# Five score banks, norms beside the attention values, and joint Q and K sums in a cosine-similarity attention kernel

## The chip, the cores and the metric

The kernel runs on one core of a Trainium2 chip. The metric is device microseconds (us) of one execution; the median of three runs before the change is 190.02 us (189.93 to 190.08). The profile is of one execution of its own, and its numbers are used as durations.

## The reference

Eight batches of twelve heads, 512 positions of 64 elements, fp32 in and out, tau = 0.1:

```python
Q_norm = Q / (np.linalg.norm(Q, axis=-1, keepdims=True) + 1e-10)
K_norm = K / (np.linalg.norm(K, axis=-1, keepdims=True) + 1e-10)
scores = np.einsum('bhqd,bhkd->bhqk', Q_norm, K_norm) / tau
weights = np.exp(scores - np.max(scores, axis=-1, keepdims=True))
weights = weights / (np.sum(weights, axis=-1, keepdims=True) + 1e-10)
return np.einsum('bhqk,bhkd->bhqd', weights, V).astype(np.float32)
```

The scores are cosines over tau, at most 10, so the kernel leaves the maximum out.

## The kernel before

The 96 heads are taken as 48 pairs (0 to 47); a pair fills 128 partitions with two heads of 64. For each pair s the work is a chain of named operations:

- LD loads Q (s,0) and K (s,1), LV loads V: 256 KB each, all issued by SyncE (SP), in one queue and in the order written out for it. ST stores the result. For pair 0 the loads are halves, K's from ScalarE's queue.
- SQ (L368) squares Q and K in one GpSimd (POOL) instruction; VC (L575, POOL) casts V to bf16 into `vb`, whose 65th column is one.
- The sum of squares of K is made on TensorE by SSQ (L385, eight matmuls against the identity, 64 columns, into unused columns of a value bank) and finished by a VectorE reduction of 64 elements (RED, L392). That of Q is a VectorE reduction of 512 elements (RED, L396). Pairs 1 to 3 have both on TensorE; pairs 43 and 47 both on VectorE.
- NEW (L419 to L430) are the Newton steps of the inverse square root for a group of one, two or four pairs on VectorE; the norms stand in a PSUM bank of their own (`nps`).
- SCL (L451) scales Q (VectorE) and K (POOL, for some pairs VectorE); TR (L457) transposes on TensorE into `tps`; EVA (L465, VectorE) copies that to `qt`.
- SCO (L551) makes scores on TensorE: two 64x512 matmuls, one for each head, into two of the four banks of `scps`. EXP (L567) is the exponential on ScalarE (ACT) over both banks, 1024 elements, from PSUM to `et`. A pair has four of these.
- PV (L587) multiplies with V: for each head h four steps of four matmuls of 65 columns, into value bank h of `ops`; RCP (L599) and NRM (L604) on VectorE divide by the 65th column into `ob`.

One chunk, (43, 3), has its exponential as a polynomial on VectorE and POOL. The program is straight-line: `ORDER` is a table that holds for each engine the numbers of all operations in the order in which it runs them. Each engine and the SP queue work strictly in this order, and an operation waits (through semaphores) for those that it needs. SCO of a bank waits for the EXP that read it last; VC waits for its LV; PV waits for all EXP of its pair, for VC, and for the NRM that last read its bank. In the table for SP the number 197 is the load of V of pair 4, 238 or 239 that of pair 5. Buffers are rings: 17 of Q and K, 8 of loaded V, 16 of cast V.

Of the kernel before, what the change touches and what calls it, by code (L numbers as in the profile page):

```python
# [108 lines left out]
def bass_cosine_similarity_attention_kernel(  # L109
# [26 lines left out]
    et = [sb(f"et{i}", [128, NT, 2, SEQ], bf16) for i in range(R_ET)]  # L136
# [21 lines left out]
    n_ps = nc.alloc_psum_tensor("nps", [128, R_X, MOST], f32)  # L158
# [34 lines left out]

    P.add("one", "pool", "one", -100, [], lambda e: e.memset(ones[:, :], 1.0))
# [31 lines left out]
    session, attached, early = {}, {}, []  # L226
    for s, w in sorted(((s, w) for s in range(NP) for w in range(2) if on_pe(s, w)), key=lambda j: (due_red(j[0]), j)):
        at = due_red(s) + 0.3
        if s < EARLY:
            early.append((s, w))  # L230
            continue
        due, i, h = next(x for x in slots if x[0] >= at and (x[1], x[2]) not in attached)
        attached[i, h] = (s, w)
# [93 lines left out]

    def pair(s):
# [74 lines left out]
        reds = [("RED", i, w) for i in range(first[g], first[g] + sizes[g]) for w in range(2)]  # L403
# [14 lines left out]
        elif s == first[g]:  # L418
# [17 lines left out]
            for k in news(g):  # L436
                needs = [done] if k else reds + [("SCL", i, w) for i in past for w in range(2) if w == 0 or i in K_ON_DVE]
                if k == 0 and g == R_X:
# [3 lines left out]
                done = ("NEW", g, k)  # L442
                P.add(done, "dve", "new7" if k == 7 and on_dve else "new", TF - 4.9 - slack(s, M_NEW) + (M_STEP * (k - 7) if s > 8 else 0.23 * k), needs, steps[k])

        for w in range(2):
# [81 lines left out]
    def rest(s):  # L527
# [3 lines left out]
        for c in range(NT):  # L531
# [14 lines left out]
            turn = chunks.index((s, c))  # L546
            b = turn % 2

            def sco(e, c=c, b=b):
                for h in range(2):  # L550
                    last = e.matmul(  # L551
                        out=sc_ps[:, 2 * b + h, :], lhsT=qt[iqt][64 * h : 64 * h + 64, 1, c, :],
                        rhs=qt[iqt][64 * h : 64 * h + 64, 0, :, :], start=True, stop=True)
                return last

            used = [("EXP", 0, 2 * c + i, 1) for i in range(2)] if turn < NT + 2 else exps(*chunks[turn - 2])
            P.add(("SCO", s, c), "pe", "sco", T0 + 0.9 * c, [("EVA", s)] + used, sco)
            if last_pair and c == NT - 1:
                for k, (h, lo, hi) in enumerate(PIECES):
                    P.add(("EXP", s, c, k), "act", "exp1" if hi - lo == NT else "exph", T0 + 0.9 * c + 0.3 * k,  # L560
                          [("SCO", s, c)] + [key("PV", s - R_ET, i, NT - 1) for i in range(2)],
                          lambda e, c=c, b=b, h=h, q=slice(128 * lo, 128 * hi): e.activation(
                              out=et[iet][:, c, h, q], in_=sc_ps[:, 2 * b + h, q], func=ACT.Exp, scale=math.log(2.0) / UNIT if group[s] in poly_groups else inv_tau))
                continue
            P.add(("EXP", s, c), "act", "exp", T0 + 0.9 * c,
                  [("SCO", s, c)] + [key("PV", s - R_ET, h, NT - 1) for h in range(2)] + ["table"],
                  lambda e, c=c, b=b: e.activation(  # L567
                      out=et[iet][:, c, :, :], in_=sc_ps[:, 2 * b : 2 * b + 2, :],
                      func=ACT.Exp, scale=math.log(2.0) / UNIT if group[s] in poly_groups else inv_tau))
# [12 lines left out]
        for h in range(2):  # L582
            for i in range(NT):
                def pv(e, h=h, i=i):
                    for c in range(NT):
                        t = i
                        last = e.matmul(  # L587
                            out=o_ps[h][:, 65 * t : 65 * t + 65],
# [6 lines left out]
            grid = o_ps[h][:, 0 : 65 * NT].rearrange("p (t x) -> p t x", x=65)  # L595
# [230 lines left out]
```

## Time and profile before

| | |
|---|---|
| median of three runs | 190.02 us |
| span of the profiled execution | 189.64 us |
| busy, share of the span | ACT 182.2 us (96%), PE 175.8 (93%), DVE 169.5 (89%), POOL 160.7 (85%) |
| moved by DMA | 50.76 MB, mean 268 GB/s |

PE is TensorE, PEld its weight loads, DVE VectorE, ACT ScalarE, POOL GpSimd, SPq the DMA queue that SP issues. The profiled execution stands 0.38 us below the median of the runs. "L567 ACT ... x186 | 170.9, 1182 | 0.7" reads: 186 instructions of line 567 kept ACT busy for 170.9 us in all, one of them takes 1182 ns (they overlap), and ACT was idle 0.7 us in front of them.

### The profile page before, as it was taken

The numbers are of one execution on the slowest core, as the hardware profiler recorded it, in microseconds if no ns is written. First come the engines' busy times: TensorE is split into PE (matmuls) and PEld (weight loads), VectorE is DVE, ScalarE is ACT, GpSimd is POOL, SyncE is SP. The second block draws the span as 40 slices with busy tenths as digits, with TensorE's granted clock in tenths as the row PEclk, the third lists the DMA queues.
The fourth block names the chain that finished last, engine by engine and source line by source line (L and its number), as shares of the span: only waits on it lengthen the run. The fifth ranks groups of instructions, "written<-read, shape, count | busy, mean of one in ns | idle before, by whom it ended". The sixth has DMA issues, their size and how long they took to land.

```text
span 189.6 us, 6661 instructions
## 1 busy us (share of the span) xinstructions
PE 175.8 (93%) x2705; PEld 111.0 (59%) x2705; DVE 169.5 (89%) x541; ACT 182.2 (96%) x215; POOL 160.7 (85%) x149
## 2 busy tenths in 40 slices
PE   8798899999999999999899989999999899899992
PEld 2455456566665666666466656556666566555652
DVE  1779999999999999999899998999989999998752
ACT  5699999999999999999999999999999999999993
POOL 5599998999999999999999999999999994594000
PEclk9979999999999999999999999999999999999999
DMA  5999999998997898899999999996983062200655
GB/s 163 340 352 350 349 348 370 365 367 256 301 363 253 246 337 296 258 351 309 368 379 319 359 360 368 361 341 194 313 295 119 3 221 79 94 0 3 203 188 168
DMA packets 52446, 50.76 MB, mean 268 GB/s; under 512 B 3136, under 2 KB 52416, under 8 KB 52416
## 3 DMA queue, kind: packets, MB, share of 16 engines
q1 hardware_dynamic: 51984, 50.02, 80.1%
q8 instruction: 21, 0.34, 0.7%
q10 hardware_dynamic: 432, 0.33, 0.5%
q14 instruction: 9, 0.07, 0.1%
HBM read 37.75 MB, written 12.58 MB: 265 GB/s over the span
## 4 chain that ended last, share of the span: by engine, by line
ACT 73%; PE 8%; DMA 5%; POOL 5%; DVE 3%; SPq 2%; issue 1%; DVEq 0%
ACT et L567 73%; DMA out_dram<-ob 3%; DMA qk<-in_Q_dram 3%; PE ops L587 2%; PE scps L551 2%; POOL sq L368 2%; POOL vb L575 2%; POOL qn L451 2%; PE ops L385 1%; SPq L345 1%; PE tps L457 1%; PE scps L540 1%; DVE ob L604 1%; SPq L342 0%; PE ops L619 0%
## 5 line engine op out<-in xcount | busy, mean ns | idle before, releaser
L567 ACT ACTIVATE et<-scps 128x1024 bf16<-128x1024 f32 x186 | 170.9, 1182 | 0.7 <-PE scps L551 0.6
L368 POOL TENSOR_TENSOR sq<-qk 128x1024 bf16<-128x1024 f32 x44 | 82.6, 1893 | 0.2 <-DMA qk<-in_K_dram 0.2
L551 PE MATMUL scps<-qt 64*128 64x512 bf16 x374 | 73.0, 386 | 7.0 <-ACT et L567 4.1
L587 PE MATMUL ops<-vb,et 128*128 128x65 bf16 x1504 | 75.7, 195 | 1.0 <-DVE ob L604 0.6
L587 PEld LDWEIGHTS ops<-vb,et 128*128 128x128 bf16 x1504 | 57.3, 98 | 30.4 <-issue 18.4
L451 POOL TENSOR_TENSOR qn<-qk,rk 128x512 bf16<-128x512 f32 x38 | 39.2, 1042 | 7.1 <-DVE rk L426 7.0
L604 DVE TENSOR_TENSOR ob<-ops,rd 128x256 f32<-128x256 f32 x94 | 39.1, 420 | 1.5 <-DMA out_dram<-ob 0.8
L451 DVE TENSOR_TENSOR qn<-qk,nps 128x512 bf16<-128x512 f32 x56 | 36.9, 679 | 0.7 <-ACT nps L412 0.6
L465 DVE COPY qt<-tps 128x1024 bf16<-128x1024 bf16 x47 | 32.2, 684 | 0.8 <-PE tps L457 0.6
L457 PE MATMUL tps<-ident,qn 128*128 128x128 bf16 x376 | 32.3, 221 | 0.3 <-DVE qn L451 0.2
L551 PEld LDWEIGHTS scps<-qt 64*128 64x128 bf16 x374 | 18.4, 92 | 23.7 <-ACT et L567 8.3
L396 DVE TENSOR_REDUCE xs<-sq 128x8 f32<-128x512 bf16 x46 | 30.5, 673 | 0.2 <-POOL sq L368 0.2
L575 POOL TENSOR_SCALAR vb<-vf 128x512 bf16<-128x512 f32 x48 | 28.9, 619 | 0.0
L457 PEld LDWEIGHTS tps<-ident,qn 128*128 128x128 bf16 x376 | 21.8, 98 | 10.0 <-issue 5.0
L599 DVE RECIPROCAL rd<-ops 128x4 f32<-128x4 f32 x94 | 16.3, 176 | 5.0 <-PE ops L587 3.8
L385 PE MATMUL ops<-sq,ident 128*128 128x64 bf16 x384 | 19.5, 196 | 0.2 <-DVE qt L298 0.2
L385 PEld LDWEIGHTS ops<-sq,ident 128*128 128x128 bf16 x384 | 14.7, 99 | 4.3 <-issue 3.0
L392 DVE TENSOR_REDUCE xs<-ops 128x8 f32<-128x64 f32 x46 | 9.7, 210 | 0.8 <-PE ops L385 0.7
L419 DVE TENSOR_TENSOR ts<-xs,nps 128x32 f32<-128x32 f32 (+2 forms) x34 | 6.6, 194 | 0.6
L426 DVE SCALAR_TENSOR_TENSOR nps<-ts,nps 128x32 f32<-128x32 f32 (+3 forms) x34 | 6.7, 196 | 0.5
L422 DVE SCALAR_TENSOR_TENSOR ts<-ts,nps 128x32 f32<-128x32 f32 (+2 forms) x34 | 6.5, 192 | 0.4
L362 POOL TENSOR_TENSOR sq<-qk 128x512 bf16<-128x512 f32 (+1 forms) x5 | 4.7, 954 | 2.4 <-DMA qk<-in_K_dram 2.1
(60 smaller groups left out, 52.8 us busy)
## 6 DMA issues: line engine op xcount, KB each, us to landing
vf<-in_V_dram SPq DMA_DIRECT2D x48, 256.0 KB, 6.2
qk<-in_Q_dram SPq DMA_DIRECT2D x47, 256.0 KB, 5.2
qk<-in_K_dram SPq DMA_DIRECT2D x47, 256.0 KB, 6.2
out_dram<-ob SPq DMA_DIRECT2D x47, 256.0 KB, 5.7
qk<-in_Q_dram SPq DMA_DIRECT2D x2, 128.0 KB, 2.7
qk<-in_K_dram ACTq DMA_DIRECT2D x2, 128.0 KB, 2.9
out_dram<-ob SPq DMA_DIRECT2D x1, 128.0 KB, 1.7
out_dram<-ob ACTq DMA_DIRECT2D x1, 64.0 KB, 1.8
```

What stands on the lines that cost most here:

```text
L368: lambda e: e.tensor_tensor(out=sqf, in0=data, in1=data, op=ALU.mult))
L385: last = e.matmul(out=o_ps[bank][:, 320:384], lhsT=ident[:, :], rhs=sq[iqs][:, 8 * w : 8 * w + 8, 8 * k : 8 * k + 8], start=(k == 0), stop ...
L396: lambda e, w=w, dst=dst: e.tensor_reduce(out=dst, in_=sq[iqs][:, 8 * w : 8 * w + 8, :], axis=AX.X, op=ALU.add))
L451: lambda e, w=w, r=r: e.tensor_tensor(out=qn[iqn][:, w].rearrange("p t h d -> p h t d"), in0=qk[iq][:, w].rearrange("p h (t d) -> p h t d" ...
L457: last = e.transpose(t_ps[:, w, t, :], qn[iqn][:, w, t].rearrange("p h d -> p (h d)"), ident[:, :])
L465: lambda e: e.tensor_copy(out=qt[iqt][:, :, :, :].rearrange("p w t x -> p (w t x)"), in_=t_ps[:, :, :, :].rearrange("p w t x -> p (w t x)")))
L551: last = e.matmul(out=sc_ps[:, 2 * b + h, :], lhsT=qt[iqt][64 * h : 64 * h + 64, 1, c, :], rhs=qt[iqt][64 * h : 64 * h + 64, 0, :, :], sta ...
L567: lambda e, c=c, b=b: e.activation(out=et[iet][:, c, :, :], in_=sc_ps[:, 2 * b : 2 * b + 2, :], func=ACT.Exp, scale=math.log(2.0) / UNIT i ...
L575: lambda e: e.tensor_scalar(out=vb[:, ivb : ivb + n, :, :, 0:DIM].rearrange("p n h c d -> p (n h c) d"), in0=vf[:, iv : iv + n].rearrange( ...
L587: last = e.matmul(out=o_ps[h][:, 65 * t : 65 * t + 65], lhsT=et[iet][:, c, h, 128 * t : 128 * t + 128], rhs=vb[:, ivb, h, c, :], start=(c ...
L599: lambda e, h=h, grid=grid: e.reciprocal(out=rd[io][:, h, :], in_=grid[:, :, DIM]))
L604: lambda e, h=h, grid=grid: e.tensor_tensor(out=ob[io][:, h], in0=grid[:, :, 0:DIM], in1=rd[io][:, h, :].unsqueeze(2).to_broadcast([128, N ...
```

## The change

**Exponentials.** `scps` has five banks. Up to pair 7 all stays in units of two tiles of 512; from pair 8 on `exp_groups` cuts the run of tiles into units of three and two in turn (banks 0 to 2 and 3 to 4), across pairs where `et`, now one tensor, allows it. SCO makes a unit's tiles, EXP takes them in one instruction of 1536 or 1024 elements. There are 156 EXP of these instead of 186: 60 of three tiles and 96 of two. A unit still has the same score banks as the unit before the last.

**Norms.** The bank of `nps` is given up for this. The norms of the first groups (pairs 0 to 7) stand in score bank 4 until it is needed; those of later groups in the last columns of value bank 1. So that TensorE does not write the bank while VectorE uses it, each NEW and each SCL on VectorE stands in a window: after NRM of head 1 of one pair, and PV of head 1 of the next pair waits for it (`in_window`).

**Sums.** For pairs 4 to 19 Q and K are summed together: SSQ has eight matmuls of 128 columns, RED reduces 128 elements, and the reduction of 512 goes. K of pairs 20 and 21 is now summed on VectorE, K of 43 and 47 on TensorE. All sums go to value bank 0.

**Rings and order.** The ring of Q and K has 16 buffers instead of 17, that of cast V 14 instead of 16. The tables of all engines are new.

```diff
-    sc_ps = nc.alloc_psum_tensor("scps", [128, 4, SEQ], f32)
+    sc_ps = nc.alloc_psum_tensor("scps", [128, 5, SEQ], f32)
...
-    n_ps = nc.alloc_psum_tensor("nps", [128, R_X, MOST], f32)
+    n_ps = both[:, :, 512 - 2 * MOST : 512].rearrange("p b (r x) -> p b r x", x=MOST)
+    n_head = sc_ps[:, 4, :].rearrange("p (r x) -> p r x", x=MOST)
...
+    def together(s, dst, g):
+        bank, due, before = session[s, 1]
+
+        def ssq(e):
+            for k in range(8):
+                last = e.matmul(
+                    out=o_ps[bank][:, 260:388], lhsT=ident[:, :], rhs=sq[s % R_SQ][:, :, 8 * k : 8 * k + 8],
+                    start=(k == 0), stop=(k == 7))
+            return last
...
+    def in_window(key, w, b):
+
+        if w < 0:
+            window_ops.setdefault((0, b), []).append(key)
+            return [("RED", s, 1) for s in range(1, ONE_BANK)]
+        window_ops.setdefault((w + 1, b), []).append(key)
+        return [("NRM", w, b)]
...
+        def sco(e):
+            for i, (s, c, h) in enumerate(halves):
+                last = e.matmul(
+                    out=sc_ps[:, bank + i, :], lhsT=qt[s % R_QT][64 * h : 64 * h + 64, 1, c, :],
+                    rhs=qt[s % R_QT][64 * h : 64 * h + 64, 0, :, :], start=True, stop=True)
+            return last
...
+        P.add(("EXP", u), "act", {1: "exp1h", 2: "exp", 3: "exp3"}[n], T0, [("SCO", u), "table"] + free,
+              lambda e: e.activation(out=et_all[:, at : at + n, :], in_=sc_ps[:, bank : bank + n, :], func=ACT.Exp, scale=scale))
...
+    for (s, b), keys in window_ops.items():
+        P.ops["PV", s, b, 0].needs += keys
...
-BY_VECTOR = (43, 47)
+BY_VECTOR = (20, 21)
...
-RINGS = (17, 8, 16, 6, 4, 4, 5, 8, 3)
+RINGS = (16, 8, 14, 6, 4, 4, 5, 8, 3)
...
+FIRST_WIDE = 8
+HEAD_GROUPS = 5
...
+SUMMED_TOGETHER = (4, 5, 6, 7, 8, 9, 10, 11, 12, 13, 14, 15, 16, 17, 18, 19)
...
     "sp": (
-        "6 7 69 70 108 109 10 151 152 71 195 196 110 237 238 153 271 272 197 313 314 239 347 348 273 389 390 315 "
...
+        "6 7 69 70 108 109 10 151 152 71 195 196 110 236 237 153 269 310 384 311 270 343 385 344 416 738 487 312 "
+        "386 557 596 629 415 457 526 458 456 238 488 417 668 558 150 527 197 669 271 811 345 68 770 699 597 630 "
```

Where the tables move instructions, three places matter below. The first is SP's queue. Before, V of pair 4 is its 19th transfer (the second `vf` row here; the first and third are V of pairs 3 and 5; the two halves of pair 0 count as two):

```order
L342 DMA qk5<-in_Q_dram 128x2x256
L342 DMA qk5<-in_K_dram 128x2x256
L345 DMA vf<-in_V_dram 128x2x256
L342 DMA qk6<-in_Q_dram 128x2x256
L342 DMA qk6<-in_K_dram 128x2x256
L345 DMA vf<-in_V_dram 128x2x256
L342 DMA qk7<-in_Q_dram 128x2x256
L342 DMA qk7<-in_K_dram 128x2x256
L345 DMA vf<-in_V_dram 128x2x256
```

After, V of pair 4 is the 45th transfer, the last row here; the other two `vf` rows are V of pairs 5 and 10, and `qk1` is already pair 17:

```order
L383 DMA qk11<-in_Q_dram 128x2x256
L386 DMA vf<-in_V_dram 128x2x256
L383 DMA qk12<-in_K_dram 128x2x256
L386 DMA vf<-in_V_dram 128x2x256
L383 DMA qk1<-in_Q_dram 128x2x256 [waits s_act]
L383 DMA qk14<-in_K_dram 128x2x256
L685 DMA out_0_dram<-ob2 128x2x256 [waits s_dve]
L383 DMA qk13<-in_K_dram 128x2x256
L386 DMA vf<-in_V_dram 128x2x256
```

V of pair 4 has moved 26 transfers back, behind loads of Q and K of pairs 7 to 17 and of Q of pair 19, V of pairs 5, 7, 9, 10 and 11, and the store of pair 2 (`ob2`).

The second is POOL, around the cast of V of pair 4 (it waits for `d_v4`, the arrival of that load). Before:

```order
L575 TENSOR_SCALAR vb<-vf 128x8x64 [waits d_v3]
L368 TENSOR_TENSOR sq2<-qk8 128x1024 [waits d_qk8]
L575 TENSOR_SCALAR vb<-vf 128x8x64 [waits d_v4]
L575 TENSOR_SCALAR vb<-vf 128x8x64 [waits d_v7]
L451 TENSOR_TENSOR qn2<-qk6,rk2 128x2x4x64 [waits s_pe,s_dve]
L451 TENSOR_TENSOR qn3<-qk7,rk2 128x2x4x64 [waits s_pe]
L368 TENSOR_TENSOR sq3<-qk9 128x1024 [waits d_qk9]
L368 TENSOR_TENSOR sq4<-qk10 128x1024 [waits d_qk10]
```

After:

```order
L409 TENSOR_TENSOR sq2<-qk8 128x1024 [waits d_qk8]
L409 TENSOR_TENSOR sq3<-qk9 128x1024 [waits d_qk9]
L501 TENSOR_TENSOR qn2<-qk6,rk2 128x2x4x64 [waits s_pe,s_dve]
L501 TENSOR_TENSOR qn3<-qk7,rk2 128x2x4x64 [waits s_pe]
L409 TENSOR_TENSOR sq4<-qk10 128x1024 [waits d_qk10]
L652 TENSOR_SCALAR vb<-vf 128x8x64 [waits d_v4]
L652 TENSOR_SCALAR vb<-vf 128x8x64 [waits d_v5]
L409 TENSOR_TENSOR sq5<-qk11 128x1024 [waits d_qk11]
L501 TENSOR_TENSOR qn0<-qk8,rk0 128x2x4x64 [waits s_pe,s_dve]
```

The cast has moved behind the squares of pairs 9 and 10, and the squares of pair 11 stand behind it.

The third is PE, where PV of pair 4 begins, after the transposes of pair 7 (`qn3`) and between two SCO of pair 6 (`qt2`). Before:

```order
L551 MATMUL scps<-qt2 128x512 [waits s_act]
L551 MATMUL scps<-qt2 128x512
L457 MATMUL tps<-ident,qn3 128x128 [waits s_dve]
L457 MATMUL tps<-ident,qn3 128x128 x3
L587 MATMUL ops<-vb,et4 128x65 [waits s_dve]
L587 MATMUL ops<-vb,et4 128x65 x7
L551 MATMUL scps<-qt2 128x512 [waits s_act]
L551 MATMUL scps<-qt2 128x512
```

After:

```order
L507 MATMUL tps<-ident,qn3 128x128 x4
L664 MATMUL ops<-vb,et 128x65 [waits s_dve,s_pool]
L664 MATMUL ops<-vb,et 128x65 x7
L550 MATMUL scps<-qt2 128x512 [waits s_act]
L550 MATMUL scps<-qt2 128x512
L664 MATMUL ops<-vb,et 128x65 x8
L664 MATMUL ops<-vb,et 128x65 [waits s_dve]
L664 MATMUL ops<-vb,et 128x65 x7
```

The place is the same, but PV of pair 4 now has a wait for POOL of its own, for the cast. The SCO behind it (`qt2`, third unit of pair 6) feeds the 23rd two-tile exponential.

More of the change, by code (lines that the diff above doesn't have):

```diff
@@ L437, in pair @@
                 needs = [done] if k else reds + [("SCL", i, w) for i in past for w in range(2) if w == 0 or i in K_ON_DVE]
+                if k == 0 and g > HEAD_GROUPS and slot_users[norm_bank(g)].index(g) >= 2:
+                    old = slot_users[norm_bank(g)][slot_users[norm_bank(g)].index(g) - 2]
+                    needs += [("SCL", i, w) for i in range(first[old], first[old] + sizes[old]) for w in range(2) if w == 0 or i in K_ON_DVE]
                 if k == 0 and g == R_X:
@@ L545, in rest @@
                 continue
[L546 to L569, printed above, removed]
+            for h in range(2):
+                if units[unit_of[s, c, h]][0][0] == (s, c, h):
+                    unit(unit_of[s, c, h])
         n = len(cast_with[s])
@@ L688, in on_pe, with exp_groups, norm_bank, sum_bank @@
     return 0 < s < PE_BOTH or s >= EARLY and (s not in BY_VECTOR if w else s in Q_ON_PE)
+def exp_groups(NP, NT):
+    runs, run = [], []
+    for s in range(1, NP):
+        for c in range(NT):
+            for h in range(2):
+                if (s, c) in OFF or (s, c) == (NP - 1, NT - 1):
+                    if run:
+                        runs.append(run)
+                    run = []
+                    continue
+                if run and (s % RINGS[6] == 0 and run[-1][0] != s or s == FIRST_WIDE and run[-1][0] != s):
+                    runs.append(run)
+                    run = []
+                run.append((s, c, h))
+    if run:
+        runs.append(run)
+    runs.append([(NP - 1, NT - 1, 0), (NP - 1, NT - 1, 1)])
+    units, odd = [], 0
+    for run in runs:
+        best = {(0, odd): (0, None)}
+        for n in range(len(run)):
+            for o in range(2):
+                if (n, o) not in best:
+                    continue
+                most = 2 if o or run[0][0] < FIRST_WIDE or run is runs[-1] else 3
+                for k in range(1, most + 1):
+                    if n + k <= len(run):
+                        cost = best[n, o][0] + (1 if k > 1 else 1.5)
+                        if (n + k, 1 - o) not in best or cost < best[n + k, 1 - o][0]:
+                            best[n + k, 1 - o] = (cost, (n, o, k))
+        ends = (0,) if run[-1][0] == FIRST_WIDE - 1 else (0, 1)
+        at = min(((len(run), o) for o in ends if (len(run), o) in best), key=lambda x: best[x][0])
+        path = []
+        end = at[1]
+        while best[at][1] is not None:
+            n, o, k = best[at][1]
+            path.append((run[n : n + k], (2 if run[0][0] < FIRST_WIDE else 3) * o))
+            at = (n, o)
+        units += path[::-1]
+        odd = end
+    return units, {x: u for u, (halves, bank) in enumerate(units) for x in halves}
+def norm_bank(g):
+    return 0 if g in FIRST_BANK else 1
+def sum_bank(g):
+    return 0
 def late(s):
```

158 lines of the change are left out of this document (113 added, 45 removed), and 155 rows, old and new, of the table ORDER.

## The prediction

> **What bounds the kernel now.** First the page's busy times, the chain that ended last and the waits (engine, tile, line, what it waited for: us in total, times, longest).
>
> ```profile
> span 189.6 us, 6661 instructions
> PE 175.8 (93%) x2705; PEld 111.0 (59%) x2705; DVE 169.5 (89%) x541; ACT 182.2 (96%) x215; POOL 160.7 (85%) x149
> ACT 73%; PE 8%; DMA 5%; POOL 5%; DVE 3%; SPq 2%; issue 1%; DVEq 0%
> ```
>
> ```profile
> ACT et L567 <- PE scps L551: 0.6, 2, 0.3
> PEld scps L551 <- ACT et L567: 8.3, 26, 0.8
> PE scps L551 <- ACT et L567: 4.1, 16, 0.5
> ```
>
> ScalarE bounds it: 96% busy, 73% of the chain, and its exponentials waited for scores only twice. TensorE waits for freed score banks, 42 times. But it is not far ahead, and nor are the others. Stretches of the span (length, then busy time and instructions of PE, PEld, DVE, ACT, POOL, TensorE clock, DMA share, GB/s):
>
> ```profile
> 15.00:75.00 60.00, 57.21 (x932) 37.24 (x930) 58.50 (x208) 60.00 (x66) 58.29 (x49) 1.00 0.99 322
> 105.00:180.00 75.00, 71.45 (x1108) 45.33 (x1106) 70.10 (x208) 75.00 (x83) 62.68 (x55) 1.00 0.62 206
> ```
>
> From 15 to 75 us four engines are over 95% busy and the DMA share is 0.99. An operation that comes late there has little cover; after 105 us DMA and GpSimd have room. So the reader should ask what ScalarE gains, and then what in the first 75 us is made later. Early DMA, in stretches again:
>
> ```profile
> 0.00:11.00 11.00, 8.92 (x56) 3.75 (x56) 5.19 (x14) 7.14 (x20) 6.19 (x15) 0.90 0.81 266
> 11.00:20.00 9.00, 8.16 (x114) 5.19 (x113) 8.23 (x33) 8.60 (x12) 8.80 (x8) 0.94 1.10 349
> 20.00:30.00 10.00, 8.73 (x142) 5.43 (x141) 9.61 (x36) 10.00 (x12) 8.73 (x10) 1.00 1.11 350
> 30.00:36.00 6.00, 6.00 (x100) 3.89 (x97) 5.90 (x20) 6.00 (x7) 6.00 (x6) 1.00 1.09 366
> ```
>
> The transfers are saturated from 11 us on: 266 x 11 + 349 x 9 + 350 x 10 + 366 x 6 GB/s x us give 2.93 + 3.14 + 3.50 + 2.20 = 11.8 MB by 36 us. This is what the new queue order meets.
>
> **The change part by part.** *Fewer exponentials: a gain.* The elements stay; 30 instructions go. What one costs beyond its elements, from starts on ScalarE (start, length in us):
>
> ```profile
> 16.81 4.70 ACT L567 ACTIVATE et<-scps 128x1024 bf16<-128x1024 f32 x5
> 21.33 1.10 ACT L567 ACTIVATE et<-scps 128x1024 bf16<-128x1024 f32 x1
> 184.96 1.32 ACT L562 ACTIVATE et<-scps 128x512 bf16<-128x512 f32 x3
> 185.43 0.85 ACT L562 ACTIVATE et<-scps 128x256 bf16<-128x256 f32 x2
> L567 ACT ACTIVATE et<-scps 128x1024 bf16<-128x1024 f32 x186 | 170.9, 1182 | 0.7 <-PE scps L551 0.6
> ```
>
> Five of 1024 elements take 21.33 - 16.81 = 4.52 us, 0.904 each; one of 512 takes 185.43 - 184.96 = 0.47. Twice 0.47 less 0.904 is 0.04 us fixed. By ends instead: the last three instructions, 1024 elements together, take 1.32 us against 1.18 for one, 0.07 for each extra one. I take 0.05: 30 x 0.05 = 1.5 us gained (bounds 0.04 and 0.07: 1.2 to 2.1). The mean step, 170.9 / 186 = 0.919, holds 0.015 more in small stalls; those are assumed to stay.
>
> The Trainium skill ("ScalarE: Activation LUTs", What ACT_TABLE_LOAD costs) gives an ACTIVATE 186 ns beside its elements, of which back-to-back ones overlap by 93. That leaves 93 ns for each, so by an estimate from that page 30 would save 2.8 us, and the sum below would end at 192.7. The rows above show half of it.
>
> *V of pair 4 comes late: the loss.* Its load goes from 19th to 45th place. Before, the 19th and the 45th were issued here, and a load of V lands a median 6.2 us after issue:
>
> ```profile
> 11.52 0.71 SPq L345 DMA_DIRECT2D vf<-in_V_dram  x1
> 32.37 0.60 SPq L608 DMA_DIRECT2D out_dram<-ob  x1
> vf<-in_V_dram SPq DMA_DIRECT2D x48, 256.0 KB, 6.2
> ```
>
> Up to and with the 45th, 45 transfers' worth are moved: 43 of 0.262 MB, pair 0's two halves here and its two on ScalarE's queue, 11.8 MB. By the stretches above that is 36.1 us, the earliest at the present rate. Issued at 32.4 and 6 us in flight, it would be 38.4. The store of pair 2 ahead of it holds the queue until its NRM is done, so less is in flight beside it: I take 37.0 (36.1 to 38.4; at the best stretch's 366 GB/s from 11 us on, 11 + 8.87 / 0.366 = 35.2).
>
> Who wants it, and when: GpSimd reaches the cast behind the square of pair 10. Before (start, length):
>
> ```profile
> 23.18 1.78 POOL L575 TENSOR_SCALAR vb<-vf 128x512 bf16<-128x512 f32 x3
> 26.79 1.20 POOL L575 TENSOR_SCALAR vb<-vf 128x512 bf16<-128x512 f32 x2
> 29.25 2.04 POOL L451 TENSOR_TENSOR qn<-qk,rk 128x512 bf16<-128x512 f32 x2 [1.26 <-DVE rk L426]
> 31.25 3.74 POOL L368 TENSOR_TENSOR sq<-qk 128x1024 bf16<-128x1024 f32 x2
> 34.97 1.20 POOL L575 TENSOR_SCALAR vb<-vf 128x512 bf16<-128x512 f32 x2
> ```
>
> The two squares of 31.25 are those of pairs 9 and 10, done at 34.97, behind five casts; after, two casts stand there. So GpSimd is at the cast by 34.97 - 3 x 0.6 = 33.2 us, or 31.9 if the wait of 1.26 does not come. It then stands still 4 to 5 us, and all behind it with it.
>
> On TensorE the PV of pair 4 stands in front of the SCO for the 23rd exponential. Before, that exponential started at 34.23:
>
> ```profile
> 34.23 1.03 ACT L567 ACTIVATE et<-scps 128x1024 bf16<-128x1024 f32 x1
> 126.66 0.39 PE L551 MATMUL scps<-qt 64*128 64x512 bf16 x2
> 126.98 0.43 PE L587 MATMUL ops<-vb,et 128*128 128x65 bf16 x8
> 127.25 0.39 PE L385 MATMUL ops<-sq,ident 128*128 128x64 bf16 x8
> ```
>
> Load 37.0, cast 0.6, eight PV matmuls 0.3 (127.25 - 126.98), SCO 0.32 (126.98 - 126.66) and its tail 0.1: 38.3, so ScalarE stands idle 38.3 - 34.2 = 4.1 us. Landing at 36.1 or 38.4 makes it 3.2 or 5.5; at 35.2, 2.3. Nothing covers it: ScalarE has only the scores of two units, and TensorE runs in order.
>
> *What is late next.* Behind the cast GpSimd does the cast of pair 5 (0.6) and the square of pair 11:
>
> ```profile
> L368 POOL TENSOR_TENSOR sq<-qk 128x1024 bf16<-128x1024 f32 x44 | 82.6, 1893 | 0.2 <-DMA qk<-in_K_dram 0.2
> ```
>
> It ends at 37.6 + 0.6 + 1.9 = 40.1. The joint sum of pair 11 stands before the SCO of the 25th exponential; with 0.46 for it (eight of 64 columns: the 0.39 of the last row above less 0.16, by which the PV row is longer than its step; twice that) and 0.4 for SCO that one starts at 41.0 instead of 38.3 + 2 x 0.9 = 40.1: 0.9 more. Afterwards GpSimd lags and can catch up only slowly (58.29 of 60 us busy); casts and squares until about pair 14 are planned tightly. I put 0.5 on that (0 to 2).
>
> *More work on TensorE.* Joint sums have 128 columns instead of 64: 0.23 us more for each of 16 pairs. The third tile of a unit shares its rows with the first:
>
> ```profile
> 6.55 0.60 PE L540 MATMUL scps<-qt 64*128 64x512 bf16 x2 [0.18 <-DVE qt L298]
> ```
>
> Two matmuls on the same rows took 0.60 us where two on different rows take 0.39, so a third costs 0.21; a unit of three and one of two 0.32 + 0.53 = 0.85 against 2.5 x 0.32 = 0.80, 0.05 more for each of 60. In pairs 8 to 19 that is some 0.3 us a pair; TensorE has 60 - 57.21 = 2.8 us in 60, 0.17 a pair. Over by 0.13 on 12 pairs: 1.6 us, of which much lies under GpSimd's lag just counted. I take 0.5 (0 to 2.5).
>
> *Less on VectorE, and its windows.* Reductions of 673 ns go for 16 pairs, those of 210 grow to about 280:
>
> ```profile
> L396 DVE TENSOR_REDUCE xs<-sq 128x8 f32<-128x512 bf16 x46 | 30.5, 673 | 0.2 <-POOL sq L368 0.2
> L392 DVE TENSOR_REDUCE xs<-ops 128x8 f32<-128x64 f32 x46 | 9.7, 210 | 0.8 <-PE ops L385 0.7
> L451 DVE TENSOR_TENSOR qn<-qk,nps 128x512 bf16<-128x512 f32 x56 | 36.9, 679 | 0.7 <-ACT nps L412 0.6
> L604 DVE TENSOR_TENSOR ob<-ops,rd 128x256 f32<-128x256 f32 x94 | 39.1, 420 | 1.5 <-DMA out_dram<-ob 0.8
> ```
>
> That frees 16 x 0.6 = 9.6 us of VectorE. It is not on the chain, so the gain is nothing by itself; it pays for the windows. In a window NRM (0.42), four Newton steps (0.2 each) and a scaling (0.68) must pass between PV of head 1 and PV of the next pair: 1.9 us with RCP, beside a pair's 3.6 on ScalarE. TensorE has about 2.2 us in between (three SCO 1.1, PV of head 0 0.55, eight transposes of 128 columns like a joint sum 0.46), so it waits little while VectorE comes on time. Queued behind a waiting PV is the next SCO, and behind that ScalarE. I take 0.5 us in all (0, hidden, to 0.3 on each of 40 pairs, 12). Pairs 20, 21, 43 and 47 exchange their reductions: 0. Shorter rings: 0, hidden by loads issued well before use after 105 us.
>
> **Sum.** On the profiled execution: 189.6 - 1.5 + 4.1 + 0.9 + 0.5 + 0.5 + 0.5 = 194.6. The median stands 0.4 above the profile: 195.0. The terms after 41 us overlap, TensorE waiting for GpSimd in the same gaps; I take 0.6 off and forecast **194.4 us**.
>
> **Rivals.**
> *DMA is in time (faster).* Place: the same cast, now without a wait. It needs 11.8 MB by 32 us, 8.87 MB in 21 us, 422 GB/s. Then 190.0 - 1.5 = 188.5. For it: nothing in the trace moves that fast; against it: a DMA share of 1.1 at 350. It decides from a landing before 32.5. The Trainium skill ("DMA: Bandwidth & Descriptors", Measured) has 425 GB/s for 16 MB with the pair's other core idle; the rows' best, 366, does not reach it, and by that page's figure the load would land at 31.9 and the time be this rival's. Chance 0.08.
> *The wait is partly eaten.* V lands at 35.2, 2.3 us idle, and GpSimd's lag costs nothing: 190.0 - 1.5 + 2.3 = 190.8. Chance 0.09.
> *TensorE and the windows take over.* If VectorE is late in its windows by 0.3 us in half of the 40 wide pairs (6 us), on top of 4.1: 190.0 - 1.5 + 4.1 + 6 = 198.6. For: both engines are over 95% busy until 75 us; against: VectorE is freed of 9.6 us just there. Chance 0.13.
> *The change does not do what it says*: wide exponentials save nothing. Then 194.4 + 1.5 = 195.9, inside the forecast's range.
>
> **How the numbers follow.** The forecast, with the last rival in it, has 0.70; its own range is 191.8 to 197.5. With the partly eaten wait below and the first half of the TensorE case above, 191.0 to 198.0 leaves out 2 in 10. What a measurement of this kernel can tell from no change is about 0.2% (0.4 us). Faster: 0.08 and 0.02 of the partly eaten case, 0.10; same: 0.03; slower: 0.87.
>
> **What would show it.** Right: GpSimd's cast line idle for some 4 us, released by the load of V, and ScalarE idle 3 to 5 us in one piece between 33 and 40 us, the chain there running through DMA, cast, PV and SCO; exponentials of 1536 elements 1.33 us apart; later idle of ScalarE small. Wrong: ScalarE without a gap there (the load is in time), or many gaps of 0.2 to 0.5 us from 45 us on released by PE scores, with PE waiting for VectorE's scaling and Newton steps (the windows).

## The result and the profile after

The changed kernel takes 202.74 us (median of six executions) against 190.05 for the kernel before on the same chip: ratio 1.0651, interval 1.0615 to 1.0687, 12.4 us slower. The forecast was 194.4 (191.0 to 198.0): the sign is right, the size is not. Some executions of any of these kernels show a lower granted clock and take some 3 to 4 us more; they are left out of the ratios and of the differences below (without them the changed kernel takes 202.5), and the rows are of an undisturbed execution of the changed kernel (202.64 us). Its page: span, busy time, shares of the chain that ended last, and the exponentials' line.

```profile
span 200.7 us, 6635 instructions
...
PE 179.6 (89%) x2705; PEld 110.7 (55%) x2705; DVE 167.4 (83%) x525; ACT 183.1 (91%) x185; POOL 160.9 (80%) x149
...
POOL 37%; PE 21%; ACT 13%; DVE 10%; DMA 8%; issue 7%; SPq 3%; POOLq 0%
...
L579 ACT ACTIVATE et<-scps 128x1024 bf16<-128x1024 f32 (+1 forms) x156 | 171.8, 1204 | 11.8 <-PE scps L550 11.5
```

ScalarE does the same work but has fallen from 73% of the chain to 13%; GpSimd leads with 37%, though it is busy for 160.9 us as before (160.7). An engine that gains weight on the chain and no work is one that waits. Busy and idle of the exponentials are 171.8 + 11.8 = 183.6, before 170.9 + 0.7 = 171.6: these 12.0 us are the loss. (The spans differ by some 11 us only, because the profiled execution of the kernel before began these exponentials 1.2 us later, at 13.85 against 12.66 us.)

All of GpSimd's waits for a load after the first 14 us (start, length, what ran, in brackets the idle time ahead of it and what ended it):

```profile
20.80 3.74 POOL L409 TENSOR_TENSOR sq<-qk 128x1024 bf16<-128x1024 f32 x2 [1.86 <-DMA qk<-in_K_dram]
38.38 1.20 POOL L652 TENSOR_SCALAR vb<-vf 128x512 bf16<-128x512 f32 x2 [4.69 <-DMA vf<-in_V_dram]
96.76 1.89 POOL L409 TENSOR_TENSOR sq<-qk 128x1024 bf16<-128x1024 f32 x1 [1.25 <-DMA qk<-in_Q_dram]
121.03 1.89 POOL L409 TENSOR_TENSOR sq<-qk 128x1024 bf16<-128x1024 f32 x1 [1.56 <-DMA qk<-in_K_dram]
126.43 1.89 POOL L409 TENSOR_TENSOR sq<-qk 128x1024 bf16<-128x1024 f32 x1 [1.33 <-DMA qk<-in_Q_dram]
150.74 1.20 POOL L652 TENSOR_SCALAR vb<-vf 128x512 bf16<-128x512 f32 x2 [1.93 <-DMA vf<-in_V_dram]
161.33 1.89 POOL L409 TENSOR_TENSOR sq<-qk 128x1024 bf16<-128x1024 f32 x1 [0.66 <-DMA qk<-in_K_dram]
```

By the order of the table these are K of pair 6, V of pair 4, Q of 29, K of 37, Q of 36, V of 46 and K of 46. The kernel before has one such wait there, of 0.2 us. The forecast had one too: the second row. ScalarE's larger gaps stand a few us behind them:

```profile
23.73 2.90 ACT L579 ACTIVATE et<-scps 128x1024 bf16<-128x1024 f32 x3 [0.64 <-PE scps L550]
27.21 8.68 ACT L579 ACTIVATE et<-scps 128x1024 bf16<-128x1024 f32 x9 [0.57 <-PE scps L550]
40.13 1.02 ACT L579 ACTIVATE et<-scps 128x1024 bf16<-128x1024 f32 x1 [4.25 <-PE scps L550]
41.67 1.02 ACT L579 ACTIVATE et<-scps 128x1024 bf16<-128x1024 f32 x1 [0.51 <-PE scps L550]
43.29 8.92 ACT L579 ACTIVATE et<-scps 128x1024 bf16<-128x1024 f32 x9 [0.60 <-PE scps L550]
...
106.43 18.37 ACT L579 ACTIVATE et<-scps 128x1536 bf16<-128x1536 f32 x16 [0.65 <-PE scps L550]
125.60 2.37 ACT L579 ACTIVATE et<-scps 128x1536 bf16<-128x1536 f32 x2 [0.80 <-PE scps L550]
129.36 1.45 ACT L579 ACTIVATE et<-scps 128x1536 bf16<-128x1536 f32 x1 [1.40 <-PE scps L550]
```

1.2 us belong to K of pair 6 (the first two rows), 5.4 to V of pair 4 (the next three), and 4.0 to the later ones, three smaller gaps of 0.26 to 0.47 us behind 129 us among them. The releaser named is TensorE's scores every time; only GpSimd's rows tell which load is behind it.

Why are the later loads late, when DMA has room? What the queue waits for (engine, line, releaser: us, times, longest), in the changed kernel and then in the kernel before, and a stretch of the changed kernel (columns as in the prediction), with the casts that end the wait in it and the load that was held:

```profile
SPq L386 <- POOL vb L652: 24.0, 10, 5.4
```

```profile
SPq L345 <- POOL vb L575: 18.0, 10, 4.6
```

```profile
85.00:88.00 3.00, 3.00 (x44) 1.80 (x43) 2.93 (x11) 3.00 (x4) 2.96 (x3) 1.00 0.47 157
87.43 1.78 POOL L652 TENSOR_SCALAR vb<-vf 128x512 bf16<-128x512 f32 x3
88.08 0.37 SPq L386 DMA_DIRECT2D vf<-in_V_dram  x1
```

The queue stood 24 us at loads of V whose buffer GpSimd had not cast yet. The kernel before stands 18 us at such loads without a late one, so the sum alone does not tell; what counts is which loads stand behind. At 85 to 88 us DMA moves 157 GB/s with work in the queue: V of pair 25 waits there for its buffer, and Q of pair 29 stands five places behind it. The new table makes this wait itself: V of pair 25 takes the buffer of V of pair 17 (the ring has 8), which is the transfer directly ahead of it, so the queue stands until that one, issued at 82.9 us, has landed and been cast. In the kernel before the two are 32 places apart. K of 37 and Q of 36 stand in the same way behind V of 30, six places after V of 22 whose buffer it takes, and behind V of 33. GpSimd then waits for them. How far a load itself has moved does not show this: K of pair 37 is the 134th transfer in both tables.

### The profile page after: what moved, and what is told of

It is laid out like the page before. It is cut to its first block, busy times and chain, and to the rows that moved or that the text cites. A ratio compares the mean times of both kernels' runs of the same rounds, so it can differ in the third digit from the quotient of the medians.

```text
span 204.3 us, 6635 instructions
## 1 busy us (share of the span) xinstructions
PE 184.7 (90%) x2705; PEld 113.6 (56%) x2705; DVE 167.3 (82%) x525; ACT 183.0 (90%) x185; POOL 160.9 (79%) x149
## 4 chain that ended last, share of the span: by engine, by line
ACT 27%; POOL 27%; PE 27%; issue 8%; DMA 5%; DVE 3%; SPq 2%; POOLq 0%
ACT et L579 27%; POOL sq L409 16%; PE scps L550 10%; PE ops L664 9%; POOL qn L501 5%; POOL vb L652 5%; PE tps L507 4%; DMA qk<-in_Q_dram 3%; DMA qk<-in_K_dram 3%; PE ops L349 2%; PE ops L430 1%; SPq L383 1%; POOL sq L403 1%; DVE ob L681 1%; DVE qn L501 1%
## 5 line engine op out<-in xcount | busy, mean ns | idle before, releaser
L579 ACT ACTIVATE et<-scps 128x1024 bf16<-128x1024 f32 (+1 forms) x156 | 171.8, 1207 | 15.8 <-PE scps L550 15.4
L409 POOL TENSOR_TENSOR sq<-qk 128x1024 bf16<-128x1024 f32 x44 | 82.9, 1893 | 11.0 <-DMA qk<-in_K_dram 5.9
L550 PE MATMUL scps<-qt 64*128 64x512 bf16 x374 | 76.2, 397 | 5.6 <-ACT et L579 1.6
L501 POOL TENSOR_TENSOR qn<-qk,rk 128x512 bf16<-128x512 f32 x38 | 39.3, 1042 | 7.6 <-DVE rk L471 7.4
L681 DVE TENSOR_TENSOR ob<-ops,rd 128x256 f32<-128x256 f32 x94 | 39.1, 420 | 1.3
L501 DVE TENSOR_TENSOR qn<-qk,ops 128x512 bf16<-128x512 f32 x46 | 31.0, 682 | 0.7
L676 DVE RECIPROCAL rd<-ops 128x4 f32<-128x4 f32 x94 | 16.0, 176 | 12.5 <-PE ops L664 8.8
L441 DVE TENSOR_REDUCE xs<-sq 128x8 f32<-128x512 bf16 x30 | 20.0, 674 | 2.7 <-POOL sq L409 2.7
L430 PE MATMUL ops<-sq,ident 128*128 128x64 bf16 x256 | 13.2, 197 | 2.4 <-POOL sq L409 2.3
L430 PEld LDWEIGHTS ops<-sq,ident 128*128 128x128 bf16 x256 | 10.1, 100 | 5.3 <-POOL sq L409 3.2
L349 PE MATMUL ops<-sq,ident 128*128 128x128 bf16 x128 | 10.6, 231 | 2.2 <-POOL sq L409 1.3
L349 PEld LDWEIGHTS ops<-sq,ident 128*128 128x128 bf16 x128 | 8.0, 103 | 3.2 <-POOL sq L409 2.7
L437 DVE TENSOR_REDUCE xs<-ops 128x8 f32<-128x64 f32 x30 | 6.1, 205 | 1.2 <-PE ops L430 1.2
L501 DVE TENSOR_TENSOR qn<-qk,scps 128x512 bf16<-128x512 f32 x10 | 6.6, 682 | 0.7 <-ACT scps L457 0.6
L356 DVE TENSOR_REDUCE xs<-ops 128x16 f32<-128x128 f32 x16 | 4.5, 280 | 2.9 <-PE ops L349 2.9
```

Of the source, the lines that this page charges most:

```text
L349: last = e.matmul(out=o_ps[bank][:, 260:388], lhsT=ident[:, :], rhs=sq[s % R_SQ][:, :, 8 * k : 8 * k + 8], start=(k == 0), stop=(k == 7))
L409: lambda e: e.tensor_tensor(out=sqf, in0=data, in1=data, op=ALU.mult))
L430: last = e.matmul(out=o_ps[bank][:, 320:384], lhsT=ident[:, :], rhs=sq[iqs][:, 8 * w : 8 * w + 8, 8 * k : 8 * k + 8], start=(k == 0), stop ...
L441: lambda e, w=w, dst=dst: e.tensor_reduce(out=dst, in_=sq[iqs][:, 8 * w : 8 * w + 8, :], axis=AX.X, op=ALU.add))
L501: lambda e, w=w, r=r: e.tensor_tensor(out=qn[iqn][:, w].rearrange("p t h d -> p h t d"), in0=qk[iq][:, w].rearrange("p h (t d) -> p h t d" ...
L550: last = e.matmul(out=sc_ps[:, bank + i, :], lhsT=qt[s % R_QT][64 * h : 64 * h + 64, 1, c, :], rhs=qt[s % R_QT][64 * h : 64 * h + 64, 0, : ...
```

## The experiments

Theory L: late loads alone, that is SyncE's order, make the loss. Theory T: TensorE's extra work and the norm windows do.

**All loads by need.** Only SyncE's table differs: loads sorted by the time at which their square or cast wants them, stores behind their last scaling.

```diff
- LV,3 LD,6,0 LD,7,0 LD,9,0 LD,7,1 LD,6,1 LD,8,0 LD,9,1 LD,8,1 LD,10,1 LD,19,0 LD,12,0 LV,7 LV,9 ...
+ LD,6,0 LD,6,1 LD,7,0 LD,7,1 LV,3 LD,8,0 LD,8,1 LD,9,0 LD,9,1 ST,0 LD,10,1 LD,10,0 LV,4 LV,5 ...
```

> The changed kernel with another order on SyncE's queue alone: each load stands by the time at which its square or cast wants it, each store behind its last scaling; the other four engines' orders are untouched. Theory L (late loads): in the changed kernel's trace every idle time of ScalarE above 0.3 us between 20 and 170 us goes back to one of six loads that landed after GpSimd stood ready for them (K of pair 6, V of pair 4, Q of 29, K of 37, Q of 36, K of 46); the gaps behind them sum to 14.7 us. So 202.7 - 14.7 = 188.0, range 187.5 to 190.5, and GpSimd's waits for loads under 1 us in all. Theory T (TensorE's extra work and the norm windows): the gaps are only shown at loads, the engines are too full, and the time stays at or above 198.

190.04 us, ratio to the kernel before 0.9975 (0.9937 to 1.0013). The whole loss is gone with one queue's order, so T falls as the cause of the loss. From its waits and its page:

```profile
SPq L386 <- POOL vb L652: 2.0, 5, 0.7
```

```profile
L579 ACT ACTIVATE et<-scps 128x1024 bf16<-128x1024 f32 (+1 forms) x156 | 170.4, 1210 | 1.2 <-PE scps L550 0.9
```

But it is not 188.0: 170.4 + 1.2 = 171.6, the sum of the kernel before to the digit. The 1.5 us of 30 saved instructions are there and are lost again, before 75 us: adding up, from start to start, what each exponential's step has above 0.904 us (two tiles) or 1.330 (three), ScalarE's small stalls up to 75 us are 3.3 us against 1.0 in the kernel before, and behind 75 us 1.7 against 2.0.

**V of pair 4 back; the five others forward.** Two halves of the same repair.

```diff
- ... LD,13,1 LV,4 LD,17,1 ...          (45th)
+ ... LD,6,0 LV,4 LD,7,0 ...            (19th)
```

> The changed kernel with V of pair 4 alone put back from the 45th to the 19th place of SyncE's queue. Theory L: the 3.33 and 1.17 us in which ScalarE idled behind it go, and K of pair 6, now one place later, costs 0.5 more: 202.7 - 4.5 + 0.5 = 198.7 (197.7 to 199.5). Theory T: the lag returns in the next stretch, under 2 us gained, 200.7 or more.

199.14 us (198.8 for the differences), ratio 1.0463 (1.0420 to 1.0506): 3.7 gained, as L had it.

```diff
- LD,7,0 LD,9,0 LD,7,1 LD,6,1 ...    LV,25 ST,12 ... LD,29,0 ...    LV,30 ... LD,37,1 ... LD,36,0 ...
+ LD,6,1 LD,7,0 LD,9,0 LD,7,1 ...    LD,29,0 LD,31,1 ...            LD,37,1 LD,36,0 LV,30 ...
```

> The changed kernel with the five late loads of Q and K (K of pair 6, Q of 29, K of 37, Q of 36, K of 46) moved forward by 3 to 20 places, V of pair 4 left late. Theory L: the gaps behind those five sum to 2.5 + 3.05 + 4.0 + 0.7 = 10.2 us; V of pair 4 then stalls GpSimd the longer, since GpSimd reaches its cast up to 2 us earlier: 202.7 - 10.2 + 0 to 2 = 192.5 to 194.5. Theory T: 200 or more.

200.06 us, ratio 1.0519 (1.0465 to 1.0573): a miss, 2.5 gained and not 10, and by the number alone what T expected; the kernel by need has already shown that the order of the loads suffices. The 10.2 us came from a profile of another execution of the changed kernel (206.35 us), whose later gaps were longer than those above: there the five have 4.8 us. And GpSimd, no longer late for K of pair 6, now stands longer at the cast of V of pair 4 (5.88 instead of 4.69 us; ScalarE's gap is 5.13 instead of 4.25). V of pair 46 stays late here, with 1.75 us of GpSimd's time.

**V of pair 4 late, nothing else.**

```diff
- ... LD,10,1 LD,10,0 LV,4 LV,5 ... LD,14,0 LD,14,1 ST,3 LV,7 ...
+ ... LD,10,1 LD,10,0 LV,5 ... LD,14,0 LD,14,1 LV,4 ST,3 LV,7 ...
```

> The first kernel of this call (all loads by need) with V of pair 4 alone made late again: it goes behind the loads of Q and K of pair 14, 12 places, to land at about 37 us. Theory L: ScalarE stands still from where its exponential would begin (34.0) to landing + 1.3 us (cast, PV, scores): 4.3, and 0.9 at the next joint sum, so 5.2 above the first kernel of this call, 193.2 if that one takes 188.0. Theory T: nothing or under 1 us above it, since GpSimd's lag lies under TensorE's.

199.49 us, ratio 1.0499 (1.0467 to 1.0532): 9.4 above the kernel by need, where 5.2 was expected. The load landed at 39.3, later than aimed at. Its rows:

```profile
39.31 1.21 POOL L652 TENSOR_SCALAR vb<-vf 128x512 bf16<-128x512 f32 x2 [7.80 <-DMA vf<-in_V_dram]
```

```profile
41.19 1.02 ACT L579 ACTIVATE et<-scps 128x1024 bf16<-128x1024 f32 x1 [7.20 <-PE scps L550]
42.73 1.02 ACT L579 ACTIVATE et<-scps 128x1024 bf16<-128x1024 f32 x1 [0.51 <-PE scps L550]
44.67 1.02 ACT L579 ACTIVATE et<-scps 128x1024 bf16<-128x1024 f32 x1 [0.92 <-PE scps L550]
```

GpSimd is ready at 31.5, 2.2 us earlier than in the changed kernel. So late loads don't add: V alone costs 9.4, the others alone (V back) 8.8, all together 12.5. A load lands by the queue's clock; a stall ahead of it only moves the engine's arrival closer to that landing (38.3 in the changed kernel and with the five forward, with GpSimd ready at 33.7 and at 32.4).

**The clock.** In that kernel TensorE had nothing to do from 33.1 to 40.0. Stretches of it:

```profile
34.00:35.00 1.00, 0.00 (x0) 0.00 (x0) 0.12 (x1) 0.00 (x0) 0.00 (x0) 1.00 0.97 285
35.00:36.00 1.00, 0.00 (x0) 0.00 (x0) 0.00 (x0) 0.00 (x0) 0.00 (x0) 0.67 0.98 320
36.00:40.00 4.00, 0.01 (x1) 0.01 (x1) 0.00 (x0) 0.00 (x0) 0.69 (x2) 0.50 0.72 231
40.00:45.00 5.00, 5.00 (x50) 3.21 (x50) 2.13 (x8) 2.38 (x3) 5.00 (x4) 0.50 0.00 1
45.00:46.00 1.00, 1.00 (x12) 0.47 (x11) 0.13 (x2) 0.94 (x2) 1.00 (x3) 0.71 0.02 7
```

The granted clock (third from the end) falls to half during the wait and stays there for the first 5 us of work. In the changed kernel GpSimd's square of pair 11 had ended at 41.4 when TensorE, busy without a break, came to the joint sum of that pair (L349) at 42.2:

```profile
39.54 1.89 POOL L409 TENSOR_TENSOR sq<-qk 128x1024 bf16<-128x1024 f32 x1
41.63 0.55 PE ops L664 x8
42.18 0.75 PE ops L349 x8
```

So 52 matmuls that nobody reads were put in front of the waiting PV:

```diff
+ P.add("hot", "pe", "hot", 0, [("EVA", 7)], hot)      # 52 matmuls of 256 columns into tps
+ P.ops["PV", 4, 1, 0].needs.append("hot")
```

> The kernel by need with V of pair 4 late (199.49), plus 52 matmuls of 256 columns without use on TensorE (into the bank of the transposes, read by nobody) while it waits for that V, ahead of the waiting PV. In that kernel TensorE's granted clock fell to 0.5 some 2.5 us into its idle time, and stayed there until 5 us after work came back. Theory C (clock): at full clock cast-to-exponential takes 0.8 instead of 1.3 us, the gaps of 0.51 and 0.92 us before the next two exponentials go, 2.0 us in all: 197.5 (197.0 to 198.2). Theory S (the predicted cause: GpSimd's square of pair 11 sets the next exponentials): the two gaps stay, 199.0 or more.

198.15 us, ratio 1.0442 (1.0394 to 1.0491), 1.3 less than without, or 1.1 by the two ratios, and the intervals overlap: three of its four executions take 198.0 to 198.2, those without 199.2 to 200.1. The profiled one is the fourth, 200.28 us; it lost time elsewhere, TensorE at half clock from 13.0 to 16.4 us and a gap of 0.83 us of ScalarE at 77.8 behind another late load. Around V of pair 4 the two gaps are gone, four exponentials run in one piece, and the clock stays:

```profile
41.81 4.01 ACT L579 ACTIVATE et<-scps 128x1024 bf16<-128x1024 f32 x4 [6.92 <-PE scps L550]
```

```profile
40.00:43.00 3.00, 3.00 (x49) 2.31 (x48) 0.77 (x3) 1.19 (x2) 3.00 (x3) 1.00 0.00 0
```

The gaps behind a late load are TensorE at half clock, not GpSimd's next square: TensorE does not wait for that square in either kernel without the idle matmuls. This run alone would not show it, since the idle matmuls, which end at 41.2, 1.6 us after the cast, give the square a head start too. They also use up some of the gain, so the 1.1 to 1.3 us are less than the 2.0 expected.

**K of pair 6 late, nothing else.**

```diff
- LD,6,0 LD,6,1 LD,7,0 LD,7,1 LV,3 LD,8,0 LD,8,1
+ LD,6,0 LD,7,0 LD,7,1 LV,3 LD,8,0 LD,6,1 LD,8,1
```

> The kernel with all loads by need (190.04), with K of pair 6 alone moved from the 17th to the 21st place of SyncE's queue; nothing else late. Theory L: it lands at about 20.8 us, GpSimd stands ready for its square at 18.3, so a wait of some 2.4 us, of which ScalarE sees 1.9 to 2.5 as in the changed kernel: 192 to 192.5. If GpSimd catches up before ScalarE runs out of scores: 190.0 to 190.5.

191.87 us, ratio 1.0091 (1.0058 to 1.0124): four places in the queue, 1.8 us above the kernel by need (2.2 by the two ratios), close to the 192 to 192.5 of theory L.

```profile
20.54 3.74 POOL L409 TENSOR_TENSOR sq<-qk 128x1024 bf16<-128x1024 f32 x2 [2.09 <-DMA qk<-in_K_dram]
```

**The parts of the change, with all loads by need.** First the changed kernel once more.

> The changed kernel itself, unaltered: its profile above was a disturbed one, 3.7 us above the median of its other executions. Theory L: the same six loads land late for GpSimd, GpSimd's waits for loads sum to 12 to 16 us, and ScalarE's idle time is 11 to 13 us instead of 15.8; the time is 202.0 to 203.2.

202.64 and 203.22 us, ratio 1.0672 (1.0627 to 1.0718). It is the profile shown above: seven late loads, V of pair 46 among them, with 13.3 us of GpSimd's time; 11.8 us idle on ScalarE.

Then two tiles in all exponentials, in the same places of the order:

```diff
-FIRST_WIDE = 8
+FIRST_WIDE = 49
```

> The kernel with all loads by need (190.04), but exponentials of two tiles in all pairs, 186 as before the change, in four of the five banks; the score matmuls go with them. The predicted gain of the wide exponentials was 30 x 0.05 = 1.5 us; in that kernel's trace an exponential of 1536 elements is followed 1.330 us later and one of 1024 0.904, again 0.05 fixed, yet its sum of small stalls is 5.05 us against 3.48 before the change. Theory E (eaten): what is gained at the instructions is lost as stalls behind TensorE's wider units and joint sums, the time stays within 0.5 of 190.0. Theory G (a gain that something else hides): two tiles cost 1.5 more, 191.5.

197.18 us, ratio 1.0366 (1.0338 to 1.0394): 7.1 more than with wide ones, far over both expectations. Waits of TensorE for a freed score bank, two tiles first and wide ones second, and the exponentials' line with two tiles:

```profile
PEld scps L550 <- ACT et L579: 19.7, 44, 1.1
...
PE scps L550 <- ACT et L579: 8.5, 25, 0.8
```

```profile
PEld scps L550 <- ACT et L579: 6.5, 19, 0.8
PE scps L550 <- ACT et L579: 2.0, 7, 0.5
```

```profile
L579 ACT ACTIVATE et<-scps 128x1024 bf16<-128x1024 f32 x186 | 174.7, 1037 | 3.6 <-PE scps L550 2.5
```

174.7 + 3.6 = 178.3, 6.7 over 171.6. With four banks TensorE stands at busy banks for 28.2 us instead of 8.5, and what queues behind it comes late. Part of that is the order, which was written for units of three; the kernel before has four banks too, and waits 8.3 + 4.1 = 12.4 us for them in an order of its own. So this prices the fifth bank in this order, not against the kernel before.

Without the joint sums:

```diff
-SUMMED_TOGETHER = (4, 5, ..., 19)
+SUMMED_TOGETHER = ()
```

> The kernel with all loads by need (190.04), but without the joint sums: Q of pairs 4 to 19 reduced on VectorE again (16 reductions of 0.67 us), K's sums of 64 columns on TensorE. The prediction took TensorE's added work at 0.5 us (0 to 2.5) and VectorE's relief at nothing by itself. If TensorE's columns are what stalls ScalarE from 15 to 60 us (eight stalls of 0.16 to 0.64 us in that kernel, most of them right behind a joint sum), 189.5 or less; if VectorE's 9.6 us are needed for the windows, 191 or more.

194.26 and 194.45 us (two executions, no interval): 4.3 more.

```profile
ACT et L579 <- PE scps L550: 4.1, 11, 0.6
```

ScalarE's gaps stand nearly all between 20 and 75 us; in that stretch TensorE's transposes, PVs and scores wait for VectorE. VectorE's relief was not spare time. The 16 reductions were given new places in VectorE's order, so part of the 4.3 us can be that order.

With two tiles and all norms in the freed fifth bank, no windows:

```diff
-HEAD_GROUPS = 5
+HEAD_GROUPS = 99
- yg = (n_head[:, g, ...
+ yg = (n_head[:, g % 8, ...
```

> The two-tile kernel of this call, in which the fifth score bank is then free: all norms are kept there, as those of the first six groups are, so that no Newton step or scaling waits for a window between two PVs and no PV for them. The prediction took the windows at 0.5 us (0 to 12). If they cost that, 0.5 below the two-tile kernel; the rival that TensorE and the windows take over had 6 us on it; if GpSimd and ScalarE cover them wholly, within 0.4 of the two-tile kernel.

197.16 us, ratio 1.0402 (1.0331 to 1.0474), against 197.18. That does not show that the windows cost nothing. In the profiled execution without windows TensorE's clock is at half between 8 and 11 us and the exponentials start at 13.60 instead of 12.51, and then:

```profile
L579 ACT ACTIVATE et<-scps 128x1024 bf16<-128x1024 f32 x186 | 174.3, 1037 | 2.8 <-PE scps L550 1.8
```

174.3 + 2.8 = 177.1 against 178.3 with windows: by this one pair of profiles they cost some 1.2 us in the two-tile kernel. In the kernel with wide exponentials their price was not measured.

**Two tries to beat both kernels.** One shifted entries of four tables of the kernel by need by a few places, by the rows' durations, to take away its stalls.

> The kernel with all loads by need (190.04), with the orders of GpSimd, VectorE, TensorE and SyncE shifted by a few places to take away the eight stalls of 0.16 to 0.64 us that its trace shows before 77 us (most of them ScalarE behind a joint sum or a transpose; one, 0.64 us, behind the square of pair 15, for which GpSimd stood at two casts). If those stalls are the price of the order and not of TensorE's work, 2 us less in the best case and about 1 by the durations of the rows: 188.0 to 189.3, faster than both kernels. If TensorE's columns themselves set them, 189.8 to 190.4.

193.77 us, ratio 1.0171 (1.0124 to 1.0219): a miss, slower than both expectations. By the starts of the exponentials the stalls up to 75 us are 3.3 us, as in the kernel by need, so these shifts did not take them away; new gaps of 1.24 and 0.80 us came at 179 and 182, the first behind PV of pair 43, which waits for the polynomial. The other looked at the one wait for a load that was left:

```profile
45.25 1.89 POOL L409 TENSOR_TENSOR sq<-qk 128x1024 bf16<-128x1024 f32 x1 [1.06 <-DMA qk<-in_K_dram]
```

```diff
- ST,3 LV,7 ST,4 LV,8 LV,9 LD,15,0 LD,15,1 ST,5
+ ST,3 LV,7 LD,15,0 LD,15,1 ST,4 LV,8 LV,9 ST,5
```

> The kernel with all loads by need (190.04), with Q and K of pair 15 moved ahead of one store and two loads of V. In that kernel one load after the start still lands late: K of pair 15, GpSimd waits 1.06 us for it and ScalarE idles 0.51 some 3 us later, its largest gap. The store held SyncE's queue for 1.6 us ahead of it. Theory L: that gap goes and nothing else comes late: 189.5, which would be 0.3 to 0.6% under the kernel before. If the gap is only shifted to the next joint sum: 190.0.

189.74 us against 190.93 for the kernel before, measured beside it, ratio 0.9943 (0.9913 to 0.9974): 0.6% faster. In the other comparisons the kernel before took 190.05 to 190.45, and against those the gain is 0.2 to 0.4%. ScalarE runs in one piece from 44 us to its last whole exponential, and the exponentials' busy and idle time is 170.7 instead of 171.6:

```profile
44.35 138.85 ACT L579 ACTIVATE et<-scps 128x1024 bf16<-128x1024 f32 x123 [0.16 <-PE scps L550]
```

```profile
L579 ACT ACTIVATE et<-scps 128x1024 bf16<-128x1024 f32 (+1 forms) x156 | 170.1, 1213 | 0.6 <-PE scps L550 0.4
```

## Why the prediction was right or wrong

- *V of pair 4 comes late: the loss.* Right in place and mechanism: landing at 37.0 (36.1 to 38.4), measured 38.3; GpSimd still for 4 to 5 us, measured 4.69; ScalarE idle 4.1, measured 4.25. That the sizes agree so well is partly luck. The prediction has GpSimd at the cast by 33.2, or 31.9 without one wait; it came at 33.7, but with 1.86 us of waiting for K of pair 6 in it, which the prediction did not have. With the other loads in time it is there at 31.5 and, with the landing at 39.3, stands 7.80 us, and ScalarE 7.20.
- *What is late next*, 0.9: two gaps, 0.51 and 0.60. The size is right by luck, since the cause is another. The square of pair 11 was done before TensorE came to it; TensorE was at half clock, which the prediction did not consider.
- *Casts and squares until about pair 14*, 0.5: one gap of 0.16 us from 44 to 105 us, which the kernels with the load in time have too. Nothing.
- *Fewer exponentials*, -1.5. The instruction is as priced. Two starts of 1536 and one of 1024 elements in the kernel by need:

```profile
92.15 1.46 ACT L579 ACTIVATE et<-scps 128x1536 bf16<-128x1536 f32 x1
93.48 1.04 ACT L579 ACTIVATE et<-scps 128x1024 bf16<-128x1024 f32 x1
94.39 1.48 ACT L579 ACTIVATE et<-scps 128x1536 bf16<-128x1536 f32 x1
```

  1.33 and 0.91 us: 1.5 x 0.904 - 1.33 is 0.03 for the half instruction saved, 0.05 an instruction. The kernel's sum did not show it (171.6 twice) until K of pair 15 came in time. The rival that wide exponentials save nothing was right on the time of the kernel by need.
- *More work on TensorE* 0.5, *windows* 0.5, the 0.6 taken off: with the loads in time, change and kernel before are equal, so TensorE's extra work, the windows and all small stalls together eat about the 1.5 and no more. How it splits was not measured; in the two-tile kernel the windows are 1.2 by one pair of profiles. With RCP (0.18) a window's chain adds up to 2.1 us and not 1.9, which leaves next to nothing of TensorE's 2.2.
- The sum with 93 ns for each instruction that is saved ends at 193.1, 1.3 under the forecast; 192.7 leaves out the 0.4 from profile to median.
- **The step that failed** is the choice to follow only the transfer that moved most, and to put all other loads at nothing for the reason given with the rings: *"Shorter rings: 0, hidden by loads issued well before use after 105 us"*. The rings are not at fault, since the kernel by need keeps them and takes 190.04. What fails is the reason: the new table permutes the whole queue. Six more loads came late, four of them after 105 us, where DMA does have room: the queue has not, because it stands at a load of V whose buffer isn't free, and everything behind stands too. Of ScalarE's loss the prediction had 5.0 us, 4.1 and 0.9 for V of pair 4, which measured 5.4; it had nothing for K of pair 6 (1.2) and for the later loads (4.0). K of pair 6 had moved by three places only; four places cost 1.8 us in the kernel by need. And without these V of pair 4 alone would have cost more, 9.4.
- *Rivals.* "DMA is in time" and "the wait is partly eaten" fell with the landing at 38.3. "TensorE and the windows take over" gave 198.6, the nearest time, by the wrong mechanism: the loads alone bring it all back.

## What to carry to other kernels

Where a queue's order is changed, price every entry against the time at which its reader wants it: place times the time of one transfer, plus each wait of the queue ahead of it. Free bandwidth is no cover for a load that stands behind a waiting one, and a load placed soon after the one whose buffer it takes makes the queue wait by itself. And when a bottleneck's share of the chain falls while another engine's rises at equal busy time, look for what that engine waits for, at every one of its waits.

## What the runs showed of the hardware

TensorE's clock. The changed kernel, around the cast of V of pair 4:

```profile
39.00:40.00 1.00, 0.94 (x10) 0.44 (x10) 0.00 (x0) 0.00 (x0) 1.00 (x2) 0.63 1.09 383
40.00:43.00 3.00, 3.00 (x38) 2.29 (x36) 1.33 (x4) 2.05 (x2) 3.00 (x3) 0.55 1.09 375
```

Between full and half clock, a mean of 0.63 over 1 us puts the fall at 39.3, and 0.55 over 3 us the return at 42.7; TensorE was idle from 35.1 to 39.1. With V alone late, idle from 33.1 to 40.0, the rows shown there give 35.3 and 45.6 in the same way. It fell 4.2 us after the last matmul in the one (0.2 us after work was back) and 2.2 us after it in the other, and came back 3.6 and 5.6 us after work did. The Trainium skill (TensorE: Matmul & The Clock Gate, HAM oscillation) warns of idle gaps over some 3.4 us. Both gaps are longer, and behind both the clock was at half, so the trace agrees; the fall after 2.2 us is earlier than that figure. What was not expected is that a late load costs more than its wait: some 1.1 to 1.3 us of 9.4 by the run with idle matmuls, whose interval overlaps that of the run without.

Left open: which of TensorE's added columns, windows and stalls before 75 us eats the 1.5 us, and how the loss of the two-tile kernel splits between the bank and the order.
